# Two-layer diffusion backbone on one core: a token transform over half the rows, context tokens first in a norm, and a new split of work between engines

## The chip, the cores and the metric

The kernel runs on one core of one Trainium2 chip. A core has TensorE for matrix products (PE in the views; PEld is its weight load), VectorE (DVE) and ScalarE (ACT) for elementwise work, GpSimd (POOL) for elementwise work and for issuing transfers, and SyncE (SP), which here only issues transfers. The metric is the device time of one execution in microseconds, as the median of three runs.

## The reference

Two layers work on 512 latent tokens and 256 context tokens, each a vector of 1024 values. The arithmetic is single precision throughout.

```python
h  = modulate(rmsnorm(x, g1), sh1, sc1)          # adaLN: shift and scale from c @ w_ada
z  = h @ w_in                                    # nine groups of 256 columns
mix = concat([mixer_a(z), mixer_b(z), mixer_c(z), diff_attention(z)])
x  = x + gt1 * (mix @ w_out)
h  = modulate(rmsnorm(x, g2), sh2, sc2)
a, b = split(h @ w_up)                           # 2816 columns each
x  = x + gt2 * ((silu(dwconv3(a)) * b) @ w_down)

def mixer_c(z):                                  # 4 heads of 64 columns, tokens x columns
    f = group(z, G_CF).reshape(B, N, HEADS, HEAD_DIM)
    return jnp.fft.fft2(f, axes=(1, 3), norm='ortho').real
```

Context tokens use the same weights with their own modulation, read only context tokens, and are dropped in layer 1 after the attention has read their keys and values. So layer 0 has T = 768 tokens (latent 512, context 256) and layer 1 has T = 512. `mixer_c` is a two-dimensional discrete Fourier transform over tokens and head columns, of which the real part is kept.

## The kernel before, in words

Single precision is built from three products of numbers with a shortened mantissa (the type fp32r): every operand is kept as a high part and a low part (`wh`, `wl` for weights, `hhi`, `hlo` for the normed tokens, `mhi`, `mlo` for the mixers' output, `fhi`, `flo` and `pqh`, `pql` in the Fourier mixer), and `passes` gives high x high, low x high, high x low. Weights come from HBM as blocks `wr` of 128 x 1024 ("units") on SP's queue; ScalarE casts them to `wh`, and VectorE or GpSimd subtracts (`wl = wr - wh`), as `wl_engine` says. While `state["norm"]` is set, from the second group of tokens of a norm until its tokens are normed, that is GpSimd.

The program is written as strands (generators). A planner, `Sched`, runs through them when the program is built: it gives each operation a price, keeps a clock for each engine and locks for what two engines share, and so writes one fixed order for every engine. The number in `K.spawn(..., n)` is a strand's rank. The prices and ranks are numbers in the source, so a small edit moves many instructions. At run time an engine takes its instructions strictly in that order and waits at each one for its operands.

One layer goes: first norm, projections of the nine groups, attention strands (`attend`, `attend_v`, `combine`) beside the mixers, output projection `w_o` in two passes, middle norm, feed-forward, end norm. `final_pass` makes the second half of the `w_o` product (and the last of the down projection) group by group of tokens; `post` adds the product to `x` (`x<-banks,ada,x`), squares it on ScalarE (`sq`), and sums (`ss`). `rstd_of` then needs a product on TensorE (`ss,mats`), a root, a reciprocal (`rt`) and another product (`rt,mats`). `make_h` gives for each of eight blocks k the normed tokens: `ht` on VectorE, `hhi` on ScalarE, `hlo` on VectorE. In layer 0 the groups are the latent tokens (LAT), then the context (CTXG); in layer 1 two halves of the latent tokens.

The feed-forward walks over pairs of column blocks f. Most are done as "quads", a scheme with seven instead of eight products of 256-column halves, for which `right_factors` makes sums of `hhi` and `hlo` blocks: `b1`, `b2` on GpSimd, `t13`, `t24` and others on VectorE. The pairs before `PLAIN` are done plainly, with 512-column products. GpSimd adds partial down projections to `xacc` in HBM by transfers.

`mixer_c` takes the projected group (`cf_split` makes its high and low parts), multiplies each block of 128 tokens by `d64`, the 64-point cosine and sine matrix (`d64,f`, 256 columns), and then for cosine and sine adds up over all N/128 token blocks a product with the table `dft` (`w,pq`, 258 columns for the latent tokens, 130 for the context). The adaLN values of layer 1 are made on VectorE by `ada_blocks`: a transfer of a 512 KB block `adaw` on SP's queue, then one multiplication with a running sum (`adaw<-adaw,silu`, 128 x 1024). Those of layer 0 that are needed at once are made on TensorE (`ada_pair`).

Of the kernel before, what the change touches and what calls it, by code (L numbers as in the profile page):

```python
# [17 lines left out]
SEQ = 512  # L18
# [4 lines left out]
HD = 64  # L23
# [57 lines left out]
class Sched:  # L81
# [138 lines left out]
    def mms(self, items, more=False):  # L220
# [5 lines left out]
        for o, l, r, a, b in items:  # L226
            c = max(0.06, self.n(r) * 0.000449 + 0.004)
            if r.dtype == F32:
                c *= 4 if self.n(l) > 64 else 2.1 if self.n(l) > 32 else 1.05
            cost += c  # L230
# [204 lines left out]
def build(tc, a, out):  # L435
    nc = tc.nc
    es = ExitStack()
    with es:
# [58 lines left out]
        for l in range(DEPTH):  # L497
# [9 lines left out]
            zt(G_DQ, 1)  # L507
            tk(0, G_DV)
            tk(1, G_AU)
# [8 lines left out]
            plan.append((f"dft{l}.c", a["dft"][0], 4 * NDFT))  # L518
            plan.append((f"dft{l}.s", a["dft"][1], 4 * NDFT))
# [247 lines left out]
        def batch_t(keys, h, gsets, tokset, between=None):  # L767
# [5 lines left out]
            for allowed in tokset:  # L773
                p = yield from P.get("zt", 1 if allowed[-1][0] + allowed[-1][1] <= 512 else 2, keep=KF())
                pp.append(p)
# [83 lines left out]
        def scores(l, h, qt, kts, sk, res):  # L859
# [28 lines left out]
            K.spawn(combine(l, pm, pc, s, c, res, qt), 1)  # L888
# [209 lines left out]
        def cf_split(p, T, fz, u):  # L1098
            hi = yield from S.get("fhi", F32R, keep=KM)
            lo = yield from S.get("flo", F32R, keep=KM)  # L1100
            yield from K.split(hi[:, 0:T], lo[:, 0:T], p[:, 0:T], ("act", "dve"))
            P.put(p)
            fz[u] = (hi, lo)

        def mixer_c(l, tb, fz, trip, grp, T, mix):
            tv = [tuple(w.rearrange("p (n k) -> p n k", n=4) for w in t) for t in tb]
            for u in range(2):
                yield from K.when(lambda: u in fz)
                pq, held = [], []
                for toks in trip:  # L1110
                    n = 256 * len(toks)
                    hi = yield from S.get("pqh", F32R, keep=KM)
                    lo = yield from S.get("pql", F32R, keep=KM)
                    p = yield from P.get("pq", (len(toks) + 1) // 2, keep=KF())
# [3 lines left out]
                    yield from K.split(hi[:, 0:n], lo[:, 0:n], p[:, 0:n], ("act", "dve"))  # L1118
                    P.put(p)
                    held += [hi, lo]  # L1120
                    pq += [(hi[:, 256 * i:256 * i + 256], lo[:, 256 * i:256 * i + 256]) for i in range(len(toks))]
                S.put(*fz[u])
                y = yield from S.get("cy", keep=KM)
                for c0, N, v in grp:
                    p = yield from P.get("ndft", 2 if v == 0 else 1, keep=KF())
                    o2 = 512 if v == 0 else 256
                    nt = N // 128
                    nk = 258 if v == 0 else 130
                    for m in range(2):
                        for n in range(nt):  # L1130
                            items = []
                            for j, (z, w) in enumerate(passes(pq[c0 // 128 + n], tv[m])):
                                rhs = w[:, n, 0:258] if v == 0 else w[:, n, 0:260:2]
                                items.append((p[:, o2 * m:o2 * m + nk], z[:, 128 * m:128 * m + 128], rhs,
                                              n == 0 and j == 0, n == nt - 1 and j == 2))
                            yield from K.mms(items)
                    sc = 1.0 / math.sqrt(N * HD)
                    e = yield from S.get("ce", keep=KM)
                    half = N // 2
                    yield from K.act(e[:, 0:half + 1], p[:, 0:half + 1], AF.Copy, scale=sc)  # L1140
# [6 lines left out]
                S.put(*held)  # L1147
                if u == 1:
                    unit_done(*tb)
# [94 lines left out]
        def layer(l):  # L1244
# [22 lines left out]
            pp = yield from batch_t(keys, h, [both] if l == 0 else [[LAT], [CTXG]], [grp, both, grp], second_q)  # L1267
# [14 lines left out]
            for i in range(2):  # L1282
                t = yield from S.get("v2")
                v2.append(t)
# [11 lines left out]
            yield from tok_group(G_DV, [[0, 1, 2, 3], [4, 5]], lambda p, i, toks: put_v2(p, toks, v2))  # L1296
            state["attention"] = True
            K.spawn(attend(l, not last, stk, v2, oTs, aq), 1)
            K.spawn(attend_v(l, not last, v2, oTs, aq, grp, mix), 1)
# [3 lines left out]
            K.spawn(mixer_a(l, trip, uu, vv, T, mix), 1.5)  # L1303
# [11 lines left out]
            for u in range(2):  # L1315
                p = yield from proj(G_CF, u, grp)
                K.spawn(cf_split(p, T, fz, u), 1)
# [4 lines left out]
            tb = []  # L1322
            for c in "cs":
                w = yield from unit(f"dft{l}.{c}")
                tb.append(w)
            K.spawn(mixer_c(l, tb, fz, trip, grp, T, mix), PMC)

# [28 lines left out]
            halves = [(0, SEQ // 2, 0), (SEQ // 2, SEQ // 2, 0)] if last else both  # L1356

            def final_pass(keys, ops, which, after):
# [24 lines left out]
                for gi, g in enumerate(halves):  # L1383
# [41 lines left out]
            yield from final_pass([f"wo{l}.1.{j}" for j in range(4)], mix[4:8], 2, after_mid)  # L1425
# [241 lines left out]
            def after_last(gi, g, r):  # L1667
# [9 lines left out]
                else:  # L1677
# [3 lines left out]
                    if gi == 0:  # L1681
# [157 lines left out]
```

## Time and profile before

| | |
|---|---|
| median of three runs | 1517.11 us (1516.86 to 1518.28) |
| profiled execution | 1526.69 us |
| its span in the profile | 1524.6 us |
| mean granted TensorE clock | 0.977 |
| busy: PE, PEld, DVE, ACT, POOL | 95%, 84%, 75%, 49%, 22% |
| chain that ended last | PE 67%, issue 14%, DVE 8%, DMA 5%, POOL 4% |

The span is what the profile's clock runs over; the profiled execution's own time is 2.1 us more than its span and 9.6 us more than the median. Busy time is summed over the whole program; the chain goes back from the last instruction through whatever released each step.

### The profile page before, as it was taken

The page shows a single profiled execution, that of the slowest core. Times are in us where ns is not written, and L with a number is a line of the kernel's source. Part 1 is how long each engine was busy: PE and PEld are TensorE (multiplying, and loading weights), DVE is VectorE, ACT ScalarE, POOL GpSimd, SP SyncE. Part 2 cuts the span into 40 slices and gives each one's busy share as a digit, 9 for nine tenths or more (in the row PEclk, how much of TensorE's full clock was granted, in tenths as well). Part 3 has the DMA queues.
Part 4 walks back from the last instruction along what each step waited for, and adds up shares of the span by engine and source line. Part 5 has one row for each costly group of instructions (what it writes and reads, how often), then busy time and mean ns, then how long its engine had stood idle before and what let it go on. Part 6 is the DMA issues. An engine that isn't in the chain of part 4 may idle for free.

```text
span 1524.6 us, 24194 instructions
## 1 busy us (share of the span) xinstructions
PE 1449.2 (95%) x9312; PEld 1285.9 (84%) x9312; DVE 1136.3 (75%) x1910; ACT 750.1 (49%) x1165; POOL 330.8 (22%) x336
## 2 busy tenths in 40 slices
PE   6999999998999999999998989899988999999996
PEld 4877878886888999999998878776787889999986
DVE  4737678648887878888879487787777868778774
ACT  5436466323543545455444444545534455666552
POOL 0211323006101111111010243163234011221121
PEclk9999999999999999999999989999999999999997
DMA  9584243115026578766775944344331276677563
GB/s 374 166 289 153 60 128 119 54 37 179 28 91 172 145 182 213 187 168 164 206 189 177 275 153 119 128 127 134 122 110 57 89 162 153 160 183 196 126 146 117
DMA packets 77171, 230.20 MB, mean 151 GB/s; under 512 B 10656, under 2 KB 12832, under 8 KB 76928
## 3 DMA queue, kind: packets, MB, share of 16 engines
q1 hardware_dynamic: 51264, 161.74, 31.5%
q0 software_dynamic: 25504, 66.54, 20.6%
q8 instruction: 73, 1.20, 0.3%
q14 instruction: 42, 0.34, 0.1%
q10 hardware_dynamic: 288, 0.39, 0.1%
HBM read 165.70 MB, written 51.38 MB: 142 GB/s over the span
## 4 chain that ended last, share of the span: by engine, by line
PE 67%; issue 14%; DVE 8%; DMA 5%; POOL 4%; ACT 1%; SPq 1%; POOLq 0%; DVEq 0%; ACTq 0%
PE banks L224 66%; POOL xacc L206 3%; PE banks L237 2%; DMA adaw<-in_w_ada 1%; DVE ss L276 1%; DMA adaw<-in_w_adaT 1%; DVE hlo L292 1%; DMA x<-xacc 1%; DVE wl L276 1%; SPq L195 1%; DVE ht L292 1%; DVE p L292 0%; DMA wr<-in_w_o 0%; DMA stk<-rhi 0%; DVE mx L318 0%
## 5 line engine op out<-in xcount | busy, mean ns | idle before, releaser
L266 ACT CAST wh<-wr 128x1024 fp32r<-128x1024 f32 x224 | 233.9, 1048 | 170.4 <-PE banks L224 104.0
L224 PE MATMUL banks<-hlo,wh 128*128 128x512 f32 (+2 forms) x960 | 295.8, 332 | 16.3 <-DVE hlo L292 16.2
L224 PE MATMUL banks<-hhi,wh 128*128 128x512 f32 (+2 forms) x960 | 300.4, 337 | 0.6 <-ACT hhi L256 0.6
L224 PE MATMUL banks<-hhi,wl 128*128 128x512 f32 (+2 forms) x960 | 295.1, 332 | 5.6 <-DVE wl L276 5.6
L276 DVE TENSOR_TENSOR wl<-wr,wh 128x1024 fp32r<-128x1024 f32 x186 | 228.9, 1232 | 65.1 <-ACT wh L266 64.0
L206 POOL DMA_DIRECT2D xacc<-ev x128 | 110.4, 866 | 627.2 <-ACT ev L305 621.9
L224 PEld LDWEIGHTS banks<-hlo,wh 128*128 128x128 f32 x960 | 173.8, 191 | 30.9 <-DVE hlo L292 18.8
L224 PEld LDWEIGHTS banks<-hhi,wh 128*128 128x128 f32 x960 | 173.3, 191 | 22.3 <-issue 9.7
L224 PEld LDWEIGHTS banks<-hhi,wl 128*128 128x128 f32 x960 | 173.5, 191 | 19.8 <-DVE wl L276 6.5
L224 PE MATMUL banks<-hi,wh 128*128 128x512 f32 (+1 forms) x560 | 173.1, 351 | 4.4 <-DVE x L292 3.9
L224 PE MATMUL banks<-lo,wh 128*128 128x512 f32 (+1 forms) x560 | 171.7, 348 | 0.0
L224 PE MATMUL banks<-hi,wl 128*128 128x512 f32 (+1 forms) x560 | 171.6, 348 | 0.0
L278 POOL TENSOR_TENSOR wl<-wr,wh 128x1024 fp32r<-128x1024 f32 (+1 forms) x38 | 93.9, 2474 | 296.1 <-ACT wh L266 259.6
L305 ACT ACTIVATE ev<-banks,ada 128x512 f32<-128x512 f32 x192 | 111.4, 616 | 78.8 <-PE banks L224 52.1
L224 PEld LDWEIGHTS banks<-hi,wh 128*128 128x128 f32 x560 | 97.8, 192 | 18.2 <-DVE x L292 4.1
L224 PEld LDWEIGHTS banks<-hi,wl 128*128 128x128 f32 x560 | 97.4, 192 | 14.1
L224 PEld LDWEIGHTS banks<-lo,wh 128*128 128x128 f32 x560 | 97.7, 192 | 13.5
L276 DVE TENSOR_TENSOR wr<-wr 128x512 f32<-128x512 f32 x144 | 96.2, 686 | 15.0 <-DMA wr<-in_w_up 13.9
L224 PE MATMUL banks<-th,wl 128*128 128x384 f32 (+1 forms) x288 | 89.5, 311 | 2.7 <-DVE wl L276 2.7
L224 PE MATMUL banks<-th,wh 128*128 128x384 f32 (+1 forms) x288 | 89.0, 309 | 1.5 <-ACT wh L266 1.5
L318 DVE TENSOR_REDUCE mx<-banks 128x1 f32<-128x768 f32 (+1 forms) x80 | 67.8, 848 | 30.0 <-PE banks L224 28.1
L292 DVE SCALAR_TENSOR_TENSOR x<-banks,ada,x 128x256 f32<-128x256 f32 (+1 forms) x88 | 49.7, 576 | 53.4 <-PE banks L224 31.6
(227 smaller groups left out, 3089.6 us busy)
## 6 DMA issues: line engine op xcount, KB each, us to landing
wr<-in_w_up SPq DMA_DIRECT2D x88, 512.0 KB, 4.4
adaw<-in_w_adaT SPq DMA_DIRECT2D x56, 512.0 KB, 5.1
xacc<-ev POOLq DMA_DIRECT2D x64, 384.0 KB, 9.0
wr<-in_w_dn SPq DMA_DIRECT2D x44, 512.0 KB, 4.7
xacc<-ev POOLq DMA_DIRECT2D x64, 256.0 KB, 7.7
adaw<-in_w_ada SPq DMA_DIRECT2D x40, 384.0 KB, 6.9
wr<-in_w_zt SPq DMA_DIRECT2D x24, 512.0 KB, 4.6
wr<-in_w_o SPq DMA_DIRECT2D x16, 512.0 KB, 3.7
```

Source lines behind the costliest of these rows:

```text
L195: yield from self.op([(q, cost[q], lambda q=q: eng[q].dma_start(out, in_)) for q in queues], outs, ins)
L206: yield from self.op([("pool", 0.9, lambda: self.nc.gpsimd.dma_start(out, in_, accum_op=ALU.add))], [], [in_])
L224: self.nc.tensor.matmul(o, l, r, start=a, stop=b, skip_group_check=more)
L237: self.nc.tensor.transpose(o, i, ident)
L266: opts.append(("act", 0.19 + n / 1200, lambda: self.nc.scalar.copy(out, in_)))
L276: opts.append(("dve", 0.15 + n / 960, lambda: self.nc.vector.tensor_tensor(out, a, b, op=op)))
L278: opts.append(("pool", 0.1 + n * 2.25e-3, lambda: self.nc.gpsimd.tensor_tensor(out, a, b, op=op)))
L292: lambda: self.nc.vector.scalar_tensor_tensor(out, a, s, b, op0=op0, op1=op1, **k))], outs, ins, lock)
L305: emit = dict(act=lambda: self.nc.scalar.activation(out, a, AF.Copy, scale=s), dve=lambda: self.nc.vector.tensor_scalar(out, a, s, None, o ...
L318: lambda: self.nc.vector.tensor_reduce(out, in_, axis=AX.X, op=op), [out], [in_])
```

## The change

It has five parts, and the numbers of the planner.

1. `mixer_c` uses that cosine is even and sine odd in the token index. `cf_fold`, in place of `cf_split`, adds row N-n to row n for the cosine half and subtracts it for the sine half (VectorE, the second operand read backwards; a few small copies on ScalarE), so that each half has N/2 rows. The product with `d64` is made in 128-column halves; the product with the table sums over N/256 blocks. Row N/2 is carried apart (`cmid`, eight small products in plain single precision, `cend`), and enters as a bias in two strided copies of the output. The tables of one layer are one unit instead of two.
2. The middle norm of layer 0 takes CTXG first, then LAT; the end norm of layer 0 keeps LAT first.
3. While `state["norm"]` is set, `wl` is made on VectorE.
4. In layer 1 one pair more (f = 4, 5) is plain: 96 products of 512 columns for 168 of 256.
5. Ranks and buffer counts: see the end of the diff. `LA` is how many adaLN pairs of layer 0 are asked for ahead, `NAQ` the number of `adaw` buffers, `PLATER` the rank of a strand with later adaLN pairs, `PMC`, `PATT`, `PATV`, `PGM`, `PCMB` those of the mixers and of the attention by layer. The planner's price of a narrow fp32r product gets a floor.

`ENDCTX` is false, so what hangs on it does as before.

```diff
         def wl_engine():
-            if state.get("norm") or state.get("attention") and K.T["pool"] < K.T["dve"] + WLA or len(units) >= WLU:
+            if state.get("norm"):
+                return ("dve",)
+            if state.get("attention") and K.T["pool"] < K.T["dve"] + WLA or len(units) >= WLU:
                 return ("pool",)
             return None
...
-            plan.append((f"dft{l}.c", a["dft"][0], 4 * NDFT))
-            plan.append((f"dft{l}.s", a["dft"][1], 4 * NDFT))
+            plan.append((f"dft{l}", a["dft"], 4 * NDFT))
...
-        def cf_split(p, T, fz, u):
+        def cf_fold(p, groups, fz, u):
+            T = groups[-1][0] + groups[-1][1]
+            f = yield from S.get("cf", keep=KM)
+            yield from K.copy(f[:, 0:T], p[:, 0:T], ("act", "dve"))
+            g = yield from S.get("cg", keep=KM)
...
+            for c0, N, _ in groups:
+                h = N // 2
+                rev = f[:, c0 + h + 1:c0 + N][:, ::-1]
+                yield from K.tt(g[:, c0 + 1:c0 + h], p[:, c0 + 1:c0 + h], rev, ALU.add)
+                yield from K.tt(g[:, c0 + h + 1:c0 + N], p[:, c0 + 1:c0 + h], rev, ALU.subtract)
...
-                    for i, t in enumerate(toks):
-                        yield from K.mms([(p[:, 256 * i:256 * i + 256], f[:, 128 * t:128 * t + 128], d, j == 0, j == 2)
-                                          for j, (f, d) in enumerate(passes(fz[u], d64))])
+                for i, cs in enumerate(tiles):
+                    for m, c in enumerate(cs):
+                        o = slice(256 * i + 128 * m, 256 * i + 128 * m + 128)
+                        yield from K.mms([(p[:, o], f[:, c:c + 128], d[:, 128 * m:128 * m + 128], j == 0, j == 2)
+                                          for j, (f, d) in enumerate(passes((fh, fl), d64))])
+                yield from K.mms([(p[:, 1000:1000 + len(grp)], d[:, 0:128].bitcast(F32), mid[:, 0:len(grp)], j == 0, j == 1)
+                                  for j, d in enumerate(d64)])
...
-                    nt = N // 128
+                    nt = N // 256
...
-            halves = [(0, SEQ // 2, 0), (SEQ // 2, SEQ // 2, 0)] if last else both
-
-            def final_pass(keys, ops, which, after):
+            halves = [(0, SEQ // 2, 0), (SEQ // 2, SEQ // 2, 0)] if last else [CTXG, LAT]
+
+            def final_pass(keys, ops, which, after, order):
...
-                for gi, g in enumerate(halves):
+                for gi, g in enumerate(order):
...
-PLAIN = (4, 4)
+PLAIN = (4, 6)
-LA = 3
+LA = 4
-PMC = 0.9
+PMC = (1.6, 0.9)
+PATT = (1, 0.8)
+PATV = (0.9, 1)
+PGM = (0.8, 1)
+PCMB = (1.1, 1.1)
-NAQ = 4
+NAQ = 5
-KA = 4
+KA = 2
-PLATER = 0.5
+PLATER = 1.8
```

Three places show how instructions move. The first is VectorE in the middle norm of layer 1, where the second half's `x` and the first half's `h` are made; before:

```order
L292 SCALAR_TENSOR_TENSOR x5_9983<-banks_77,ada1_92,x5_9983 128x256
L292 SCALAR_TENSOR_TENSOR hlo_10584<-ht_10585,ada1_92,hhi_10583 128x256
L292 SCALAR_TENSOR_TENSOR ht_10662<-x1_9975,acol11_96,rstd_10543 128x256
L276 TENSOR_TENSOR ss_10390<-ss_10390,sq_10625 128x256
L276 TENSOR_TENSOR ss_10390<-ss_10390,sq_10632 128x256
L292 SCALAR_TENSOR_TENSOR hlo_10661<-ht_10662,ada1_92,hhi_10660 128x256
```

and now, from the start of the same stretch:

```order
L292 SCALAR_TENSOR_TENSOR adaw_10478,ada1_92<-adaw_10478,silu_3859 128x1024
L276 TENSOR_TENSOR ss_10360<-ss_10360,sq_10485 128x256
L292 SCALAR_TENSOR_TENSOR x7_10043<-banks_77,ada1_92,x7_10043 128x256
L292 SCALAR_TENSOR_TENSOR x0_9993<-banks_77,ada1_92,x0_9993 128x256
L276 TENSOR_TENSOR ada1_92<-ada1_92,vec_81 128x1
L276 TENSOR_TENSOR ss_10360<-ss_10360,sq_10512 128x256
L292 SCALAR_TENSOR_TENSOR adaw_10522,ada1_92<-adaw_10522,silu_3859 128x1024
L292 SCALAR_TENSOR_TENSOR x1_9995<-banks_77,ada1_92,x1_9995 128x256
L314 RECIPROCAL rt_10538<-rt_10538 128x64
L276 TENSOR_TENSOR ss_10360<-ss_10360,sq_10552 128x256
L292 SCALAR_TENSOR_TENSOR x2_9997<-banks_77,ada1_92,x2_9997 128x256
L276 TENSOR_TENSOR wl_10541<-wr_10225,wh_10539 128x1024
```

Four `wl`, which GpSimd made, now stand among VectorE's norm work, the first of them in this stretch. The last six `adaw` products of layer 1's adaLN now stand in `w_o` and in this norm's first half, the last two of them here; before, four of those six were spread over the second half of the attention and two stood in `w_o`. The second place is VectorE at the end of the middle norm of layer 0, where `h` is made for the last group; before, the 512-column latent blocks come in turn with the 256-column context blocks:

```order
L314 RECIPROCAL rt_3667<-rt_3667 128x64
L292 SCALAR_TENSOR_TENSOR hlo_3661<-ht_3662,ada0_91,hhi_3660 128x512
L292 SCALAR_TENSOR_TENSOR ht_3692<-x4_2809,acol01_94,rstd_3479 128x512
L292 SCALAR_TENSOR_TENSOR ht_3687<-x0_2801,acol01_94,rstd_3654 128x256
L292 SCALAR_TENSOR_TENSOR hlo_3691<-ht_3692,ada0_91,hhi_3690 128x512
```

and now:

```order
L276 TENSOR_TENSOR wl_3648<-wr_3281,wh_3610 128x1024
L276 TENSOR_TENSOR ss_3315<-ss_3315,sq_3668 128x512
L276 TENSOR_TENSOR wl_3676<-wr_3344,wh_3656 128x1024
L314 RECIPROCAL rt_3702<-rt_3702 128x128
L292 SCALAR_TENSOR_TENSOR ht_3731<-x0_2809,acol01_94,rstd_3688 128x512
L292 SCALAR_TENSOR_TENSOR hlo_3484<-ht_3731,ada0_91,hhi_3483 128x512
L292 SCALAR_TENSOR_TENSOR ht_3754<-x1_2811,acol01_94,rstd_3688 128x512
```

All eight context blocks are done by then, two `wl` stand ahead of the last reciprocal, and `ht` and `hlo` of the latent blocks alternate, eight times. On TensorE, between the last `w_o` product and the first product with a latent `h`, there are 72 products of 256 columns with the context's `h`. The third place is VectorE at the start of layer 1's feed-forward, where the right factors of the quads (`t13`, `t24`) meet the convolution (`fy`) and the first weights; before:

```order
L292 SCALAR_TENSOR_TENSOR fy_11007<-banks_77,vec_81,fy_11007 128x511 x2
L276 TENSOR_TENSOR t13_11042<-b1_11022 128x256
L276 TENSOR_TENSOR t13_11042<-b1_11022,b2_11031 128x256
L292 SCALAR_TENSOR_TENSOR t24_11052<-t13_11042,b2_11031 128x256
L276 TENSOR_TENSOR t24_11052<-b2_11031,t24_11052 128x256
L276 TENSOR_TENSOR fy_11006<-banks_77,fy_11006 128x512
L276 TENSOR_TENSOR wl_11029<-wr_10608,wh_11008 128x1024
```

and now:

```order
L292 SCALAR_TENSOR_TENSOR fy_10997<-banks_77,vec_81,fy_10997 128x511 x2
L276 TENSOR_TENSOR wl_11008<-wr_10588,wh_10998 128x1024
L276 TENSOR_TENSOR t13_11014<-b1_10994 128x256
L276 TENSOR_TENSOR t13_11014<-b1_10994,b2_11001 128x256
L292 SCALAR_TENSOR_TENSOR t24_11042<-t13_11014,b2_11001 128x256
L276 TENSOR_TENSOR t24_11042<-b2_11001,t24_11042 128x256
L276 TENSOR_TENSOR fy_10995<-banks_77,fy_10995 128x512
L276 TENSOR_TENSOR wl_11036<-wr_10614,wh_11007 128x1024
```

The `wl` stood behind the four operations on `b1` and `b2`, and one now stands ahead of them. On TensorE, 96 plain products of the down projection now follow the plain up projection, ahead of the first quad.

## Rows read from the trace of the kernel before

**Rows 1.** Page, part 1: engine, busy us, share of the span, instructions.

```profile
PE 1449.2 (95%) x9312; PEld 1285.9 (84%) x9312; DVE 1136.3 (75%) x1910; ACT 750.1 (49%) x1165; POOL 330.8 (22%) x336
```

**Rows 2.** Waits of PE: waited for, us in total, times, longest us.

```profile
PE banks L224 <- DVE hlo L292: 16.2, 7, 4.2
PE banks L224 <- DVE wl L276: 10.9, 8, 4.1
...
PE banks L224 <- DVE ss L276: 3.8, 2, 2.0
```

**Rows 3.** Windows, PE only: stretch, length, PE busy, PEclk, DMA share, GB/s.

```profile
350.00:375.00 25.00, 18.80 (x86) 0.93 0.72 251
875.00:900.00 25.00, 18.83 (x130) 0.88 0.29 90
900.00:925.00 25.00, 25.00 (x112) 0.91 0.48 183
1125.00:1150.00 25.00, 20.88 (x166) 0.86 0.52 169
1150.00:1175.00 25.00, 23.18 (x167) 1.00 0.00 1
1175.00:1200.00 25.00, 20.27 (x79) 0.86 0.14 43
```

**Rows 4.** Timeline of POOL, then DVE, layer 0's middle norm: start us, us, operation.

```profile
349.42 2.72 POOL L278 TENSOR_TENSOR wl<-wr,wh 128x1024 fp32r<-128x1024 f32 x1
...
349.76 2.92 DVE L292 SCALAR_TENSOR_TENSOR ht<-x,acol,rstd 128x512 f32<-128x512 f32 x1
...
357.75 0.74 DVE L292 SCALAR_TENSOR_TENSOR ht<-x,acol,rstd 128x512 f32<-128x512 f32 x1
```

**Rows 5.** The same, layer 1's middle norm.

```profile
1134.70 2.42 POOL L278 TENSOR_TENSOR wl<-wr,wh 128x1024 fp32r<-128x1024 f32 x1
...
1138.16 2.35 POOL L278 TENSOR_TENSOR wl<-wr,wh 128x1024 fp32r<-128x1024 f32 x1
...
1134.24 7.09 DVE L276 TENSOR_TENSOR ss<-ss,sq 128x256 f32<-128x256 f32 x2
```

**Rows 6.** Page, part 5: operation, count, busy us, mean ns, idle before.

```profile
L276 DVE TENSOR_TENSOR wl<-wr,wh 128x1024 fp32r<-128x1024 f32 x186 | 228.9, 1232 | 65.1 <-ACT wh L266 64.0
```

**Rows 7.** Timeline of DVE, then POOL, end of layer 0's middle norm.

```profile
371.23 2.17 DVE L292 SCALAR_TENSOR_TENSOR hlo<-ht,ada,hhi 128x512 fp32r<-128x512 f32 x1
...
370.91 1.94 POOL L278 TENSOR_TENSOR b<-hhi,hlo 128x768 f32<-128x768 f32 x1 [1.75 <-DVE hlo L292]
```

**Rows 8.** Timeline of PE in layer 1, across a change of shape.

```profile
1263.27 0.40 PE L224 MATMUL banks<-hi,wh 128*128 128x512 f32 x1
1263.51 0.40 PE L224 MATMUL banks<-lo,wh 128*128 128x512 f32 x1
```

**Rows 9.** Groups of PE in the Fourier mixer by form, one of three each.

```profile
L224 PE MATMUL banks<-wh,pqh 128*128 128x258 f32 x32 | 10.1, 316 | 0.4 <-DVE pqh L269 0.4
...
L224 PE MATMUL banks<-d64h,fhi 128*128 128x256 f32 x20 | 5.9, 296 | 0.4 <-ACT aT L266 0.3
```

**Rows 10.** Timeline of PE, Fourier mixer of layer 0, back to back.

```profile
264.49 0.29 PE L224 MATMUL banks<-wl,pqh 128*128 128x258 f32 x1
...
265.32 0.29 PE L224 MATMUL banks<-wh,pql 128*128 128x258 f32 x1
...
273.29 0.30 PE L224 MATMUL banks<-wh,pql 128*128 128x130 f32 x1
...
273.65 0.30 PE L224 MATMUL banks<-wh,pql 128*128 128x130 f32 x1
```

**Rows 11.** Timeline of DVE, attention of layer 1.

```profile
954.41 1.23 DVE L292 SCALAR_TENSOR_TENSOR adaw<-adaw,silu 128x1024 f32<-128x1024 f32 x1 [3.54 <-DMA adaw<-in_w_adaT]
...
1035.96 1.22 DVE L292 SCALAR_TENSOR_TENSOR adaw<-adaw,silu 128x1024 f32<-128x1024 f32 x1 [3.88 <-DMA adaw<-in_w_adaT]
```

**Rows 12.** Timeline of PE, start of layer 0.

```profile
77.11 0.63 PE L224 MATMUL banks<-adaw,sl 128*32 128x256 f32 x6 [2.50 <-DMA adaw<-in_w_ada]
```

More of the change, by code (lines that the diff above doesn't have):

```diff
@@ L506, in build @@
             zt(G_BX, 0)
-            zt(G_DQ, 1)
+            if l == 0 or not ENDCTX:
+                zt(G_DQ, 1)
             tk(0, G_DV)
+            if l and ENDCTX:
+                zt(G_DQ, 1)
             tk(1, G_AU)
@@ L1139, in mixer_c @@
                     half = N // 2
-                    yield from K.act(e[:, 0:half + 1], p[:, 0:half + 1], AF.Copy, scale=sc)
+                    for q in range(2):
+                        yield from K.act(e[:, q:half + 1:2], p[:, q:half + 1:2], AF.Identity,
+                                         bias=ends[:, 2 * gi + q:2 * gi + q + 1], scale=sc)
                     yield from K.stt(y[:, c0:c0 + half + 1], p[:, o2:o2 + half + 1], -sc, e[:, 0:half + 1],
@@ L1266, in second_q, with values, context_values @@
                 K.spawn(rope(p, grp, res, (1, "q")), 1)
-            pp = yield from batch_t(keys, h, [both] if l == 0 else [[LAT], [CTXG]], [grp, both, grp], second_q)
+            dv = []
+            def values(toks_list, last):
+                for i in range(0 if dv else 2):
+                    w = yield from unit(f"w{l}.{G_DV}.{i}")
+                    dv.append(w)
+                while len(v2) < 2:
+                    t = yield from S.get("v2")
+                    v2.append(t)
+                for toks in toks_list:
+                    p = yield from proj_tok(dv, h, toks)
+                    K.spawn(put_v2(p, toks, v2), 1)
+                if last:
+                    unit_done(*dv)
+            def context_values():
+                yield from K.when(lambda: all((k, CTXG[0]) in h.done for k in range(8)))
+                yield from values([[4, 5]], False)
+            pp = yield from batch_t(keys, h, [both] if l == 0 else [[CTXG], [LAT]] if ENDCTX else [[LAT], [CTXG]], [grp, both, grp],
+                                    context_values if ENDCTX else second_q)
             K.spawn(rope(pp[0], grp, res, (0, "q")), 1)
@@ L1321, in layer @@
             state["h_free"] = True
[L1322 to L1326, printed above, removed]
+            tb = yield from unit(f"dft{l}")
+            K.spawn(mixer_c(l, tb, fz, grp, T, mix), PMC[l])
             if not last:
@@ L1424, in after_mid @@
                     state["norm"] = False
-            yield from final_pass([f"wo{l}.1.{j}" for j in range(4)], mix[4:8], 2, after_mid)
+            yield from final_pass([f"wo{l}.1.{j}" for j in range(4)], mix[4:8], 2, after_mid, halves)
             mix = None
@@ L1689, in layer @@
                 state["h"] = hn
-            yield from final_pass([f"dn{l}.{di + u}" for u in range(4)], [hidf[q] for q in prev], 5, after_last)
+            yield from final_pass([f"dn{l}.{di + u}" for u in range(4)], [hidf[q] for q in prev], 5, after_last, halves if last or ENDCTX else [LAT, CTXG])
         def main():
@@ L1702 @@
 QUADS = (0, 1)
-PLAIN = (4, 4)
+PLAIN = (4, 6)
 PADA = 2
-LA = 3
+ENDCTX = False
+LA = 4
 NWH = 5
```

99 lines of the change are left out of this document (56 added, 43 removed).

## The prediction

> **What bounds the kernel now.** The first view is the busy time of each engine: TensorE works 95% of the span [rows 1], so only two things can shorten the program much: fewer products, or the 5% in which TensorE stands still. The second view, its waits, says who is late. The reader is to see that the two largest are both VectorE's: `hlo`, the low part of the normed tokens, with 16.2 us in seven waits of up to 4.2, and `wl`, the weights' low part, with 10.9 us; `ss`, the norm's sum, adds 3.8 [rows 2]. The third view cuts the span into stretches of 25 us and shows where those waits lie [rows 3]. I read as lost in a stretch what TensorE was idle, plus the length times what the granted clock lacked to 1.00. That gives 6.2 + 1.75 = 8.0 us in the middle norm of layer 0 (350 to 375), 6.2 + 3.0 + 2.25 = 11.4 at the end norm of layer 0 (875 to 925), 4.1 + 3.5 = 7.6 in the middle norm of layer 1 (1125 to 1150) and 1.8 + 4.7 + 3.5 = 10.0 at the start of layer 1's feed-forward (1150 to 1200): 37 us in four places. In all four the granted clock's mean is under 1.00: behind a standstill TensorE works on at 1.2 instead of 2.4 GHz for a while, which adds to the loss.
>
> The fourth view is the timeline of the two engines that make the norm, and there lies the cause. While GpSimd works on a `wl` from 349.42 for 2.72 us, VectorE's `ht` that starts at 349.76 takes 2.92 us; the same `ht` alone takes 0.74 [rows 4]. In layer 1 two sums take 7.09 us, and end only when the second of two `wl` on GpSimd is over [rows 5]. So these operations don't run slower beside GpSimd, they stand until it has finished. The Trainium skill has this rule (SBUF — State Buffer, Who interferes with whom): a VectorE instruction with two operands in SBUF and a GpSimd instruction that reads SBUF exclude each other for the whole instruction; the trace agrees, with 2.92 for 0.74 us.
>
> **The change part by part.** *Fourier transform.* The products with the table come in three kinds of 32 at 258 columns [rows 9] and three of 8 at 130; half of them go. Back to back, seven steps take 0.83 us, 0.119 each, at 258 columns, and three take 0.36, 0.120 each, at 130 [rows 10]. That is 48 x 0.119 + 12 x 0.12 = 7.2 us less. The 60 products with `d64` (three kinds of 20, [rows 9]) stay 60 but have 128 columns instead of 256. At 130 columns a step is no shorter than at 258, so I count 0 for them. The Trainium skill speaks against that zero (TensorE: Matmul & The Clock Gate, Back-to-back issue gap): it gives about 81 ns a product at 128 columns in a sustained stream, by which an estimate would be 60 x 0.038 = 2.3 us more gain; the row of 0.120 at 130 columns differs from it, and I take the row. The eight `cmid` products in plain single precision have no row; they cost between nothing and, at two steps each, 2 us; I take 1.2, since a step doesn't shrink with columns. Sum: -6 us (-7 to -5). The fold costs VectorE about 1.5 us for each half of the heads, in a part of the attention where TensorE has other strands; without that cover it would be 6 us in all.
>
> *Middle norm of layer 1.* The four `wl` cost VectorE 1.23 us each [rows 6], 4.9 in all, and the locks go: 7.09 us for two sums that need about 0.7 each. Between the first half's `ht` and `hlo` VectorE then has two `wl` and not a standstill of some 5 us. I take the loss from 7.6 to 2.5 us: -5 (-7 to 0; 0 if the 4.9 us all land on the path).
>
> *End norm of layer 0.* The same exchange. Its first standstill, of 2.0 us on `ss` [rows 2], comes before `state["norm"]` is set and stays, with half of the lost clock. The loss goes from 11.4 to about 6.5: -5 (-7 to 0).
>
> *Middle norm of layer 0.* The locks by `wl` go here too, but the order is new. After the last `w_o` product a chain runs for the latent tokens: `x`, square, sum, product, root, reciprocal, product, `ht`, `hhi`, `hlo`. That is ten steps of 0.5 to 0.9 us, with two `wl` of 1.23 between, some 9 to 11 us. TensorE has 72 context products of 0.119, 8.6 us, in that time: 1 to 2 us are open. Then each block k gives it nine products of 512 columns at 0.24 [rows 8], 2.2 us, while VectorE and ScalarE need `ht`, `hhi`, `hlo` one behind the other, at 0.74 each [rows 4]: 2.2 without handing over, about 2.5 with it. And when two blocks are done, GpSimd makes `b1` and `b2`, 1.94 us each. Beside one of them `hlo` took 2.17 us [rows 7]. So a block takes VectorE 2.2 to 3.5 us, and eight blocks leave TensorE 0 to 10 us idle. I take 5, with the chain 6.5, against 8.0 now: -1.5 (-7 to +4).
>
> *Start of layer 1's feed-forward.* TensorE stood 4.1 us for one `wl` [rows 2], which stood in VectorE's order behind four operations on `b1` and `b2` and these behind GpSimd's lock. Now a `wl` stands ahead of them, and 96 products of 0.24, 23 us, come before the first quad, in which the right factors can be finished. The loss goes from 10.0 to 3: -7 (-10 to -2). The plain pair itself costs 96 x 0.24 - 168 x 0.119 = +3.
>
> *Ranks.* VectorE waited 3.54 and 3.88 us for an `adaw` block in the attention of layer 1 [rows 11], with the softmax behind it, and TensorE then for the softmax. The first stays where it is; the product that waited 3.88 is among those that go to `w_o`. I take -3 (-5 to +2). At the start of layer 0 the loads of later `adaw` blocks now stand behind 20 and not 12 other transfers of the queue, and TensorE already waits 2.50 us for the first of them [rows 12]: +2 (-2 to +5). The rest of the attention and of the feed-forward has the same work in nearly the same order: 0 (-4 to +5).
>
> *Sum.* -6 - 5 - 5 - 1.5 - 7 + 3 - 3 + 2 = -22.5 us. The profiled execution took 1526.7 us, 2.1 above its span and 9.6 above the median; I take the terms off the median: 1517.1 - 22.5 = 1495 us.
>
> **The rivals.** *VectorE takes the lock's place.* In the norms TensorE waits for VectorE, and this change gives it twelve `wl`, 14.8 us. If each lands on the path, the three norms gain what the locks cost less 4.9 each, which is next to nothing: the terms of 11.5 us go, and 1506 us remain. For it: `hlo` waits lead [rows 2]. Against: VectorE's idle time in the norms is what the locks take, and 7.09 for two sums is more than four `wl`.
>
> *All standstills go.* If the norms and the start of the feed-forward ran without loss, 37 us would be won there instead of 18.5: about 1477 us; with the half of that surplus 1484. Against it: `ss` at the end of layer 0 is untouched.
>
> *No gain.* The gains are taken back by waits in parts that I counted at nothing, at their upper ends (5 + 5 + 5) plus 4 in layer 0's middle norm: about 1514 us.
>
> *Slower: `adaw` blocks late in layer 1's `w_o` and norm.* Six multiplications now stand there, in VectorE's order among `x` and `ss`, and VectorE waits at each for its transfer. In the attention such waits were 3.5 to 3.9 us [rows 11]. Six of 3.9 are 23 us, each behind a product whose `x` is late, so that TensorE's buffers fill; with the clock down to 1.2 GHz behind them, as in [rows 3], another 1.75 us or more each: 34 us, and 1529 in the end. It decides from about 3.7 us for each of the six, all on the path. Against it: there is one more `adaw` buffer, so that the transfers can start earlier, and in that part fewer other loads are due.
>
> **How the numbers follow.** Chances: the forecast 0.45 (own range 1489 to 1502), VectorE in the lock's place 0.2, all standstills gone 0.13, no gain 0.1, slower 0.12. Within 0.2%, 3 us either way, a measurement of this kernel can't tell a change from none. Of "no gain" 0.07 falls within it and 0.03 on the faster side; of the slower case 0.02 falls within. Faster: 0.45 + 0.2 + 0.13 + 0.03 = 0.81; same 0.09; slower 0.10. The range leaves out the slow case and the lowest part of the quick one: 1478 to 1516.
>
> **What would show it.** Right: no operation of VectorE over 2 us in the norms but where `b1` and `b2` run; the stretches that answer to [rows 3] with clock 0.95 or more in layer 1; 60 products fewer in `w,pq`, and those with `d64` halved in columns at an unchanged step of 0.12 us. Wrong would be the step on the middle norm of layer 0 if TensorE waits there for more than 8 us on `hlo`; that on the ranks if VectorE waits on `adaw` in layer 1's `w_o`; that on the Fourier part if 128 columns step at 0.08 us, or if the fold makes TensorE wait for `fhi`. The whole would be wrong if the `wl` of the norms are what TensorE waits for: then `wl` leads the list of its waits.

## The result, and the profile after

The changed kernel takes 1490.22 us (median of four runs, 1488.47 to 1494.02), the kernel before beside it 1516.98: a ratio of 0.983 (from all runs, not from the two medians), 95% interval 0.980 to 0.987. In a second series, on another chip, it was 1489.97 against 1519.06, ratio 0.981 (0.979 to 0.984). The forecast was 1495, the range 1478 to 1516: 22 us of gain were forecast and 25 to 29 came.

The profiled execution took 1489.44 us, its span 1487.6. Busy time of the engines, as in [rows 1]:

```profile
PE 1430.4 (96%) x9196; PEld 1265.3 (85%) x9196; DVE 1118.2 (75%) x1909; ACT 745.3 (50%) x1184; POOL 297.6 (20%) x321
```

What TensorE waits for, as in [rows 2]:

```profile
PE banks L224 <- DMA adaw<-in_w_ada: 8.7, 4, 3.6
...
PE banks L224 <- DVE hlo L292: 5.3, 9, 0.9
PE banks L224 <- DVE ss L276: 4.9, 3, 1.8
...
PE banks L224 <- DVE wl L276: 3.9, 5, 1.6
```

The wait for `hlo` has gone from 16.2 to 5.3 us and its longest from 4.2 to 0.9; that for `wl` from 10.9 to 3.9. The list is now led by the transfers of layer 0's adaLN. The windows, PE only, that answer to [rows 3] (the program has moved forward by some 7 us at the end norm of layer 0, and by 22 to 29 us in layer 1's middle norm):

```profile
350.00:375.00 25.00, 22.14 (x128) 1.00 0.34 125
375.00:400.00 25.00, 22.29 (x111) 0.93 0.07 22
...
875.00:900.00 25.00, 23.14 (x151) 1.00 0.67 230
...
1100.00:1125.00 25.00, 23.22 (x192) 0.93 0.50 168
1125.00:1150.00 25.00, 23.32 (x161) 1.00 0.08 23
1150.00:1175.00 25.00, 25.00 (x110) 1.00 0.45 149
```

They are counted as in the prediction (idle time, plus length times missing clock). From 350 to 400, 2.9 + 2.7 + 1.75 = 7.3 us are lost: 3.4 of them are waits for `hlo` in layer 0's middle norm, and the rest lies behind it, in the start of the feed-forward, with a wait of 2.1 us for `fy` and the clock after it. The prediction's stretch for the kernel before ended at 375; the window behind it lost 1.3 us there:

```profile
375.00:400.00 25.00, 23.66 (x155) 1.00 0.07 22
```

The end norm of layer 0 loses about 2 us, layer 1's middle norm 1.8 + 1.75 = 3.5 (1100 to 1125, which answers to 1125 to 1150 before), and the start of its feed-forward 1.7. That is some 15 us where 38 stood. A second profile of each kernel gives 15 and 40, in other shares: the end norm of layer 0 loses 4.0 us there, and layer 1's middle norm 2.2.

This is VectorE in layer 1's middle norm now.

```profile
1114.13 0.42 DVE L276 TENSOR_TENSOR ss<-ss,sq 128x256 f32<-128x256 f32 x1
1114.46 1.22 DVE L276 TENSOR_TENSOR wl<-wr,wh 128x1024 fp32r<-128x1024 f32 x1
1115.60 0.48 DVE L292 SCALAR_TENSOR_TENSOR hlo<-ht,ada,hhi 128x256 fp32r<-128x256 f32 x1
```

The `wl` costs 1.22 us between a sum and an `hlo`, each at its own length; in [rows 5] two sums stood 7.09 us. In layer 0's middle norm the standstills are not gone, only smaller. GpSimd, then VectorE:

```profile
361.36 2.22 POOL L278 TENSOR_TENSOR b<-hhi,hlo 128x768 f32<-128x768 f32 x1 [0.69 <-DVE hlo L292]
...
362.67 1.46 DVE L292 SCALAR_TENSOR_TENSOR hlo<-ht,ada,hhi 128x512 fp32r<-128x512 f32 x1 [0.79 <-ACT hhi L256]
```

An `hlo` of 0.75 us takes 1.46 because `b` holds it. Six in a row do the same, one every 2.92 us, where TensorE's nine products need 2.2. And in the Fourier mixer, the products with `d64` in 128-column halves, back to back, and the first of those in plain single precision:

```profile
265.26 0.27 PE L224 MATMUL banks<-d64h,fhi 128*128 128x128 f32 x1
...
266.15 0.27 PE L224 MATMUL banks<-d64h,flo 128*128 128x128 f32 x1
266.26 0.33 PE L224 MATMUL banks<-cmid,d64h 128*128 128x2 f32 x2
...
266.68 0.60 PE L224 MATMUL banks<-mhi,wh 128*128 128x512 f32 x2
```

Eight steps take 0.89 us: 0.111 each, for half the columns of the 0.119 of [rows 10]. Two of the products in plain single precision take the 0.42 us from 266.26 to 266.68, so the eight of them cost some 1.7 us, where the prediction took 1.2.

### The profile page after: what moved, and what is told of

It reads as the page before. It is cut to its first block, busy times and chain, and to the rows that moved or that the text cites. A ratio compares the mean times of both kernels' runs of the same rounds, so it can differ in the third digit from the quotient of the medians.

```text
span 1487.6 us, 23938 instructions
## 1 busy us (share of the span) xinstructions
PE 1430.4 (96%) x9196; PEld 1265.3 (85%) x9196; DVE 1118.2 (75%) x1909; ACT 745.3 (50%) x1184; POOL 297.6 (20%) x321
## 4 chain that ended last, share of the span: by engine, by line
PE 67%; issue 17%; DMA 5%; DVE 5%; POOL 3%; ACT 1%; SPq 1%; POOLq 0%; DVEq 0%; ACTq 0%
PE banks L224 65%; POOL xacc L206 3%; PE banks L237 2%; DMA adaw<-in_w_ada 2%; DMA x<-xacc 1%; DVE hlo L292 1%; SPq L195 1%; DVE ht L292 1%; DMA xacc<-ev 1%; DMA adaw<-in_w_adaT 1%; DVE wl L276 1%; ACT hhi L256 0%; DVE ss L276 0%; DMA mats<-in_mats 0%; DMA wr<-in_w_dn 0%
## 5 line engine op out<-in xcount | busy, mean ns | idle before, releaser
L266 ACT CAST wh<-wr 128x1024 fp32r<-128x1024 f32 x220 | 229.7, 1048 | 192.2 <-PE banks L224 128.0
L224 PE MATMUL banks<-hhi,wh 128*128 128x512 f32 (+2 forms) x968 | 303.5, 338 | 2.9 <-DVE fy L292 2.1
L224 PE MATMUL banks<-hlo,wh 128*128 128x512 f32 (+2 forms) x968 | 300.3, 335 | 5.5 <-DVE hlo L292 5.3
L224 PE MATMUL banks<-hhi,wl 128*128 128x512 f32 (+2 forms) x968 | 298.3, 332 | 0.4 <-DVE wl L276 0.4
L276 DVE TENSOR_TENSOR wl<-wr,wh 128x1024 fp32r<-128x1024 f32 x196 | 240.3, 1228 | 74.6 <-ACT wh L266 73.9
L224 PEld LDWEIGHTS banks<-hhi,wl 128*128 128x128 f32 x968 | 173.5, 190 | 14.3 <-DVE wl L276 0.6
L276 DVE TENSOR_TENSOR wr<-wr 128x512 f32<-128x512 f32 x136 | 90.8, 686 | 13.6 <-DMA wr<-in_w_up 12.6
L278 POOL TENSOR_TENSOR wl<-wr,wh 128x1024 fp32r<-128x1024 f32 (+1 forms) x24 | 59.4, 2476 | 147.9 <-ACT wh L266 108.3
L224 PE MATMUL banks<-th,wl 128*128 128x384 f32 (+1 forms) x272 | 84.7, 311 | 1.6 <-DVE wl L276 1.6
L224 PE MATMUL banks<-tl,wh 128*128 128x384 f32 (+1 forms) x272 | 84.3, 310 | 0.0
L224 PE MATMUL banks<-th,wh 128*128 128x384 f32 (+1 forms) x272 | 84.2, 310 | 0.0
```

The source lines that it names most:

```text
L224: self.nc.tensor.matmul(o, l, r, start=a, stop=b, skip_group_check=more)
L266: opts.append(("act", 0.19 + n / 1200, lambda: self.nc.scalar.copy(out, in_)))
L276: opts.append(("dve", 0.15 + n / 960, lambda: self.nc.vector.tensor_tensor(out, a, b, op=op)))
L278: opts.append(("pool", 0.1 + n * 2.25e-3, lambda: self.nc.gpsimd.tensor_tensor(out, a, b, op=op)))
```

## The experiments

The theory: the gain is the lock, that is, VectorE's operations no longer stand behind GpSimd's `wl` in the norms, with smaller parts from the fold and the plain pair. The rivals: `wl` on VectorE costs there what the lock cost; or the new order and ranks make the gain, whatever the engine. Ratios are to the kernel before on the same chip. The changed kernel was measured on two chips, on which the kernel before took 1516.98 and 1519.06 us; some experiments ran on two others, where it took 1519.26 and 1518.32. So differences in us to the changed kernel hold to some 3 us.

**A common measure.** The changed kernel again.

> The changed kernel once more, beside the three others on one chip, so that they have a common measure. Any theory: ratio to the kernel before 0.980 to 0.987, some 1490 us.

Measured: 1489.97 us against 1519.06, ratio 0.9813 (0.9789 to 0.9837).

**The lock put back.** The order of every engine's other instructions stays as it is; only the twelve `wl` of the norms go to GpSimd.

```diff
-                yield from K.tt(lo[:, 0:n], src, hi[:, 0:n], ALU.subtract, wl_engine() or ("dve", "pool"))
+                if state.get("norm"):
+                    yield from K.op([("dve", 0.15 + n / 960, lambda: K.nc.gpsimd.tensor_tensor(...))], ...)
+                else:
+                    yield from K.tt(lo[:, 0:n], src, hi[:, 0:n], ALU.subtract, wl_engine() or ("dve", "pool"))
```

> The changed kernel with its order kept as it is, but the wl of the norms issued on GpSimd instead of VectorE. Theory (the lock: while GpSimd works on wl, VectorE's operations on two SBUF operands stand): VectorE operations of 2 to 5 us come back in the norms, and 10 to 18 us of the gain go, ratio 0.990 to 0.996. Rival (the new order and ranks made the gain, the engine of wl counts little): within 3 us of the changed kernel. Rival (VectorE is what TensorE waits for in the norms, and wl on it costs): faster than the changed kernel.

Measured: 1509.37 us, ratio 0.9943 (0.9922 to 0.9964): 19.4 us more than the changed kernel, a little over the theory's upper end. The timeline of GpSimd, then VectorE, in layer 1's middle norm shows what came back:

```profile
1123.31 1.10 POOL L195 DMA_DIRECT2D xacc<-x  x2
1124.43 2.36 POOL L594 TENSOR_TENSOR wl<-wr,wh 128x1024 fp32r<-128x1024 f32 x1
1126.73 0.56 POOL L195 DMA_DIRECT2D xacc<-x  x1
1127.31 2.35 POOL L594 TENSOR_TENSOR wl<-wr,wh 128x1024 fp32r<-128x1024 f32 x1
...
1123.96 5.99 DVE L276 TENSOR_TENSOR ss<-ss,sq 128x256 f32<-128x256 f32 x1
```

One sum that needs 0.42 us stood through two `wl` and the transfer between them, and TensorE waited 5.8 us for the `hlo` behind it. Since the order is the same, the two kernels can be compared operation by operation: VectorE's together last 23 us longer, and each of the thirteen that grew by more than 0.3 us ran beside work on GpSimd. TensorE's idle time and lost clock came back in the three norms:

```profile
350.00:375.00 25.00, 20.15 (x113) 0.86 0.53 186
875.00:900.00 25.00, 20.61 (x137) 0.93 0.31 98
...
1125.00:1150.00 25.00, 17.73 (x130) 0.80 0.37 122
```

Another explanation would be that GpSimd needs 2.4 us for a `wl` and VectorE 1.22, so that TensorE waits for the later `wl`; but its wait for `wl` is 3.4 us here against 3.9 in the changed kernel, and that for `hlo` 12.6 against 5.3. Both rivals fall: the order was the same and the time was not.

**The lock taken from the kernel before.** The mirror image, in the order of before, in which the norms have thirteen `wl`.

```diff
+                if state.get("norm"):
+                    yield from K.op([("pool", 0.1 + n * 2.25e-3, lambda: K.nc.vector.tensor_tensor(...))], ...)
```

> The kernel before with its order kept as it is, but the wl of the norms issued on VectorE instead of GpSimd. Theory (the lock): 6 to 14 us faster than before, ratio 0.991 to 0.996, and no VectorE operation of over 2 us beside a wl. Rival (1.23 us on VectorE for each wl eats what the lock costs): within 3 us of before. Rival (order): within 3 us of before.

Measured: 1504.73 us, ratio 0.9903 (0.9879 to 0.9927), 14.3 us faster. TensorE's wait for `hlo` is 5.3 us here too:

```profile
PE banks L224 <- DVE wl L276: 11.0, 8, 4.1
...
PE banks L224 <- DVE hlo L292: 5.3, 5, 1.3
```

The 4.1 us wait for `wl`, at the start of layer 1's feed-forward, is untouched. So half of the whole gain, 14 of some 27 us, is to be had from the engine of these `wl` alone, without a new order.

**The fold alone, and the change without the fold.** The first is the kernel before with the new `cf_fold`, `mixer_c` and tables; the second the changed kernel with the old ones. Both are planned anew, as any edit of the strands is.

> The kernel before with the folded token transform alone; norms, engine of wl, plain pairs, ranks and prices as before, and the order planned anew. Theory: 5 to 7 us faster, ratio 0.9955 to 0.997, all of it in the 60 products that are gone, and the 128-column products with d64 step at 0.11 to 0.12 us. Rival (the fold's VectorE and ScalarE work delays TensorE): no gain or slower, with waits for fhi or pqh of more than 2 us. Rival (a 128-column product steps at 0.08 us): 2 us more gain.

> The changed kernel with the token transform of before (whole contraction, two table units), all else as changed, the order planned anew. Theory of the prediction (60 products fewer are 6 us): 4 to 8 us slower than the changed kernel, ratio 0.985 to 0.988. Rival (as alone: the fold's gain is taken by waits for its VectorE and ScalarE work): within 3 us of the changed kernel.

Measured: alone 1520.77 us, ratio 1.0013 (0.9998 to 1.0028), no gain. Taken out of the changed kernel: 1495.84, ratio 0.9846 (0.9829 to 0.9863), 5.9 us slower. The same 60 products are worth 6 us in one order and nothing in the other. The second size is less firm than it looks. No execution without the fold (1494.29 to 1498.77) is as short as the changed kernel's longest (1494.02), but they ran on different chips, and the intervals of the two ratios overlap a little. In the profiles the difference lies in layer 0: its last `w_o` product starts at 355.3 us without the fold, and at 347.8 and 350.4 in two profiles of the changed kernel. In the profile of the fold alone TensorE has waits that the kernel before has not or hardly has:

```profile
PE banks L224 <- DVE aT L269: 3.8, 2, 3.4
...
PE banks L224 <- DVE nm L299: 2.5, 1, 2.5
```

Both belong to the attention that runs beside the mixer, the first in layer 0, the second in layer 1. Waits of over 2 us for `fhi` or `pqh`, which the rival named, aren't there. But the execution in this profile took 1514.78 us, 6 less than the median of the twelve, and one profile doesn't show what is in every execution. That the gain went into waits of the attention is possible, and not shown. Another rival stays open: the planner's floor for narrow products wasn't in this kernel, so it priced a product of 128 columns at 0.061 us, where it takes 0.111, and wrote the order by that.

**The kernel before once more.**

> The kernel before once more, for a second profile of it. If its waits in layer 1's attention for adaw blocks are the same 3.5 to 3.9 us, they belong to the kernel; if they are gone, the first profile held a slow execution's waits, and the difference of the two profiles there is no gain.

Measured: 1519.66 us, span 1517.8, against the 1524.6 of the first profile. The window in layer 1's attention in which the 3.88 us of [rows 11] lay:

```profile
1025.00:1050.00 25.00, 24.55 (x119) 1.00 0.50 155
```

In the first profile TensorE was busy for 21.12 us of that stretch and the clock 0.95. So that wait was of one execution; of the two waits of [rows 11] the other came again, with 4.07 us. The stage from layer 1's first product of weights with `h` (`w,h`) to the product `rt,mats` behind its attention, with the same number of `w_o` products in between, takes 162.9 us in this profile and 172.5 in the first, and 161.8 and 158.7 in two of the changed kernel. That is 1 to 4 us of gain. The 24 products with the table that are gone in layer 1 would be 2.9 at 0.119 each, so little or nothing is left for the ranks there.

**The ranks of before in the changed kernel.**

```diff
-LA = 4
+LA = 3
-PMC = (1.6, 0.9)
+PMC = (0.9, 0.9)
-PATT = (1, 0.8)
+PATT = (1, 1)
-PATV = (0.9, 1)
+PATV = (1, 1)
-PGM = (0.8, 1)
+PGM = (1.5, 1.5)
-PCMB = (1.1, 1.1)
+PCMB = (1, 1)
-NAQ = 5
+NAQ = 4
-KA = 2
+KA = 4
-PLATER = 1.8
+PLATER = 0.5
```

> The changed kernel with the ranks and buffer counts of before (LA, PMC, PATT, PATV, PGM, PCMB, NAQ, KA, PLATER); fold, order of the norm, wl on VectorE and plain pairs as changed. Theory (ranks are worth some 1 us, the wl and the plain pair make the gain): within 4 us of the changed kernel, ratio 0.979 to 0.985. Rival (the ranks make the gain in layer 1's attention and let the fold pay): 6 to 10 us slower than the changed kernel, ratio 0.985 to 0.988.

Measured: 1506.14 us, ratio 0.991 (0.9888 to 0.9932), 16 us slower, more than either theory. VectorE's wait for the `adaw` blocks, then TensorE's wait for the softmax on ScalarE:

```profile
DVE adaw L292 <- DMA adaw<-in_w_adaT: 18.7, 6, 7.5
...
PE banks L224 <- ACT p L256: 8.7, 5, 2.4
```

The longest of these waits, 7.5 us, lies in layer 1's attention at 1018 us, and TensorE is idle for 5.3 us of the window from 1025 to 1050 that follows. The changed kernel waits 9.9 us for these blocks, with 5.2 at the longest, and 2.0 for `p`. From layer 1's first `w,h` product to the first `ss,mats` of its middle norm this profile takes 198.0 us, the changed kernel's two 187.1 and 184.0. So most of the loss lies there, in this execution. But that execution took 1510.11 us, the most of the six (1499.36 to 1510.11), so that the 16 us come through these waits is likely, and not shown. The old ranks were made for another program and don't fit this one. What the new ranks would do in the program before was not tried, so what they are worth by themselves stays open.

**Latent tokens first, and the plain pair taken back.** One line each.

```diff
-            halves = [(0, SEQ // 2, 0), (SEQ // 2, SEQ // 2, 0)] if last else [CTXG, LAT]
+            halves = [(0, SEQ // 2, 0), (SEQ // 2, SEQ // 2, 0)] if last else both
```

> The changed kernel with the latent tokens first in layer 0's middle norm, as before; all else as changed, the order planned anew. Theory of the prediction (the turned order is worth little beside the lock): within 3 us of the changed kernel, ratio 0.979 to 0.985. Rival (context first is what covers the latent chain): 4 to 8 us slower, ratio 0.985 to 0.988. Rival (b on GpSimd stops each latent block, so that latent first is better once wl is on VectorE): 3 us faster, 0.979 or less.

```diff
-PLAIN = (4, 6)
+PLAIN = (4, 4)
```

> The changed kernel with layer 1's fifth pair as a quad again; all else as changed, the order planned anew. Theory (the 23 us of plain products cover the right factors and the first weights): a loss of some 10 us comes back at the start of layer 1's feed-forward, against 3 us fewer product time, so 4 to 8 us slower than the changed kernel, ratio 0.984 to 0.988. Rival (with the lock gone there is nothing left to cover): 3 us faster, 0.979 to 0.981.

Measured: latent first 1490.52 us, ratio 0.9817 (0.9796 to 0.9838), as the changed kernel: the order of the groups is worth nothing that can be told. Without the plain pair 1495.11, ratio 0.9843 (0.9818 to 0.9868), 5 us slower, as the theory had it. The executions (1491.87 to 1498.40) and the interval overlap with the changed kernel's, so the size is rough. The reason is another than the prediction gave. TensorE's timeline where the first quad begins:

```profile
1171.78 0.39 PE L224 MATMUL banks<-th,wh 128*128 128x256 f32 x1 [3.84 <-ACT wh L266]
```

It waits there for the cast `wh` on ScalarE, not for `wl` behind the right factors. In the changed kernel, where the plain products come first, TensorE has no such wait (25.00 us busy in each window from 1150 to 1225).

**The next lock.** From the changed kernel: the order stays, `b1` and `b2` are issued on VectorE.

```diff
-                    yield from K.tt(b1[:, 0:T], hi1[:, 0:T], lo1[:, 0:T], ALU.add, ("pool",))
+                    yield from K.op([("pool", 0.1 + T * 2.25e-3, lambda: K.nc.vector.tensor_tensor(...))], ...)
```

> The changed kernel with its order kept as it is, but b1 and b2 of the right factors issued on VectorE instead of GpSimd. Theory (the last lock in the norms is b on GpSimd, 0.7 us for each latent block): TensorE's waits for hlo in layer 0's middle norm fall from 0.73 to some 0.3 us each, and those for fy and wl beside b go; 3 to 7 us faster than the changed kernel, ratio 0.977 to 0.980. Rival (16 more operations on VectorE, 13 us, land on the path): the changed kernel's time or 3 us more.

Measured: 1481.94 us, ratio 0.9756 (0.9735 to 0.9777), 8 us faster than the changed kernel, a little more than the theory's 3 to 7. VectorE in layer 0's middle norm, then TensorE's window there:

```profile
362.94 0.75 DVE L292 SCALAR_TENSOR_TENSOR hlo<-ht,ada,hhi 128x512 fp32r<-128x512 f32 x1 [0.79 <-ACT hhi L256]
...
374.64 0.95 DVE L1526 TENSOR_TENSOR b<-hhi,hlo 128x768 f32<-128x768 f32 x1
...
350.00:375.00 25.00, 25.00 (x147) 1.00 0.36 135
```

`hlo` is back at 0.75 us, a block comes every 2.2 us, which is what TensorE needs, and TensorE stands still no more in this window. A `b` takes VectorE 0.95 us, less than half of GpSimd's 2.2.

**The wait at 77 us.** Two more versions load one, then two, of the later adaLN pairs of layer 0 ahead of the `stk` transfers of SP's queue. The edit for one:

```diff
             state["pairs"] = 8
+            for j in range(8, 9):
+                raw0[j] = yield from load_pair(j, KM)
+            state["raw0"] = raw0
...
-                        raw = yield from load_pair(8 + i, KM)
+                        if i < 1:
+                            yield from K.when(lambda: "raw0" in state)
+                            raw = state["raw0"].pop(8 + i)
+                        else:
+                            raw = yield from load_pair(8 + i, KM)
```

> The changed kernel with b1 and b2 on VectorE, and the first later adaLN pair of layer 0 loaded ahead of the stk transfers of SP's queue instead of behind 20 of them, the order planned anew with that. Theory (TensorE waits 4 us at 77 us for that pair only because of its place in the queue, and then for the clock): the loss of 12 us from 75 to 100 us falls by 6 to 9, 1473 to 1477 us, ratio 0.970 to 0.973. Rival (the next pair, still behind, is waited for instead): no faster than with b on VectorE alone, 0.975.

> The same with the first two later pairs loaded ahead of the stk transfers. Theory: as with one, or 1 to 3 us more. Rival (the two loads take the place of weight loads, whose wait costs as much): no faster than with b on VectorE alone, 0.975.

Measured: 1480.51 us, ratio 0.9746 (0.9723 to 0.9769), and 1481.93, 0.9757 (0.9733 to 0.978): neither is faster than `b` on VectorE alone. The rival of the first was right. TensorE's timeline with one pair ahead:

```profile
68.84 1.07 PE L224 MATMUL banks<-adaw,sl 128*32 128x256 f32 x16
...
88.81 2.89 PE L224 MATMUL banks<-adaw,sl 128*32 128x256 f32 x16 [5.95 <-DMA adaw<-in_w_ada]
```

The first pair now runs at 68.84 without a wait, and the one after it waits 5.95 us, since its load still stands behind the `stk` transfers. With two pairs ahead TensorE again waits once in this part, for 6.0 us. The wait has moved, not gone.

## Why the prediction was right, point by point

**The lock** was the right mechanism, and the largest part: 14 us from it alone, 19 us when it is put back. The forecast for it, with the start of the feed-forward, was 5 + 5 + 1.5 + 7 = 18.5 us; by the profiles the four places gave 38 - 15 = 23, and 25 in the second pair of profiles. The sizes were off by place. The end norm of layer 0 gained 9 us in one pair of profiles and 7 in the other, not 5: the prediction let the first standstill and half of the lost clock stay, and the standstill on `ss` stayed, but the clock's fall did not come in one profile and was 1.75 us in the other. Layer 1's middle norm was to keep 2.5 us and keeps 3.5 and 2.2, the start of the feed-forward was to keep 3 and keeps 1.7 and 1.4. In layer 0's middle norm 6.5 us were to stay, 1.5 for the chain and 5 for the blocks. The context's products covered the chain whole, and the blocks cost 3.4: the block of 2.2 to 3.5 us measured 2.92, and the experiment with `b` on VectorE shows that it was `b`. Some 3.9 us more were lost just behind the norm, on `fy` and the clock, which the prediction didn't count; they went with `b` too. One reading of the prediction was wrong without bearing on the sum: a sum of 256 columns needs 0.42 us and not 0.7, so the lock in [rows 5] was larger than it says. And of its signs one came out on the wrong side: the clock in layer 1 was to be 0.95 or more, and it is 0.93 from 1100 to 1125 in the profile shown (1.00 in the second). No VectorE operation in the norms takes over 2 us, as it said.

**VectorE takes the lock's place**, the rival at 1506 us, fell: the `wl` at 1.22 us each on VectorE cost less than they freed, twelve in the new order and thirteen in the old one. **All standstills go** came part of the way.

**The Fourier part** was forecast at -6 and is worth -5.9 in the changed kernel; that the two agree to a tenth is luck, since the difference is good to some 3 us. The prediction's own terms come to the same: 7.2 and 0.5 us less, 1.7 more for the products in plain single precision. That the halves in 128 columns gain next to nothing held: 0.111 us a step against 0.119, 60 x 0.008 = 0.5 us in all, where 0.08 had been the other possibility. But the zero for the work that the fold brings and for the new order around it doesn't hold by itself: alone the fold gained nothing, with the old ranks and the old prices.

**The plain pair** was forecast at -7 + 3 = -4 and is worth -5, within 3 or so. Its cover was right; what it covers, by the profile without it, was the cast `wh` and not only the `wl` that the prediction named.

**The ranks** were the step that failed. The prediction gave them -3 + 2, and took the -3 from waits that one profile showed [rows 11]; the second profile of before has the first of them, and only 1.0 us in place of the second. So there was hardly a gain to be had at that place. And putting the old ranks back costs 16 us, not 1: the prediction asked what the ranks do to the program before, while their size is what they keep from happening in the program after. It and the section on the change also misread one: `NAQ` is the number of attention units that may be under way, and `adaw` of layer 1 has two buffers before and after. So the argument against the slower rival, one more buffer, was empty. That rival, `adaw` blocks that hold VectorE in layer 1's `w_o` and norm, didn't come all the same: in both profiles of the changed kernel VectorE waits for none of the six. Such waits do exist in the attention, 5.2 us with the new ranks and up to 7.5 in the one profile with the old. The start of layer 0 was forecast at +2, and it came so: TensorE's wait for the adaLN pairs is 8.7 and 9.4 us after, and 6.5 and 7.8 in the two profiles before.

The parts don't add up, and can't be expected to: taken back one by one, wl (19.4), ranks (16), fold (5.9), plain pair (5) and group order (0) make 46 us, of a gain of 27. The two that were also tried alone, the wl (14) and the fold (none), are worth more with the others in place. That the sum came within 5 us is in part luck: a lock and a feed-forward that gave more than forecast stand beside ranks whose term was taken from a wait of one execution.

## What to carry to other kernels

When an operation takes several times its own length, look at what the other engine does at that moment before counting the engine as the bound; here moving twelve jobs of 2.4 us from GpSimd to VectorE gained 1.6 us for each, and thirteen in the other order 1.1, although VectorE needs 1.2 us for each of them itself. To tell an engine's part from a planner's, keep the order and change only the engine of the instruction. And take a wait into a forecast only when a second profile of the same kernel shows it again; for ranks, ask what goes wrong without them.

## What the runs showed of the hardware that was not expected

A VectorE operation on two SBUF operands that had begun to wait did not get in between two GpSimd operations. The sum at 1123.96 stood through a `wl`, a transfer's issue of 0.56 us and the next `wl`, and ended at 1129.95, 0.3 us after the second; the first of the sums of [rows 5] stood through two `wl` in the same way, in both profiles of the kernel before. The Trainium skill (SBUF — State Buffer, Who interferes with whom) calls the ports that VectorE and GpSimd share an exclusive lock. The trace agrees, with 5.99 us for 0.42; that the one who waits can be passed over a second time is what it adds. Who came first doesn't settle it here: the sum's record begins 0.47 us before the first `wl`, more than the 0.42 that it needs, while GpSimd was issuing transfers, and the profile doesn't show what held it in that time.

At 128 columns a step of TensorE took 0.111 us here. The Trainium skill (TensorE: Matmul & The Clock Gate, Back-to-back issue gap) gives about 81 ns for a sustained stream; the measurement decides for these products.
